# Three edits of order at the stage boundaries of a two-layer latent-token backbone

## The chip, the cores and the metric

The kernel runs on one core of a Trainium2 chip, in one launch. The metric is the device time of that launch in microseconds (us): 2392.98 us is the median of three runs of the kernel before (2392.16 to 2393.1). A core has TensorE (PE in the views; its weight loads are PEld), VectorE (DVE), ScalarE (ACT), GpSimd (POOL) and SyncE (SP), which issues the DMAs. Matrix products land in PSUM, which this kernel uses as eight banks of 128 x 512 float32; everything else is in SBUF.

## What is computed

Two layers work on 512 latent tokens of 1024 features; the first layer also takes 256 context tokens. Each layer is: half a feed-forward, a token mixer, half a feed-forward, each with a modulation before it and a normalization after it.

```python
def modulate(x, m, k):
    return x * (1 + m[..., 3 * k + 1, :]) + m[..., 3 * k, :]

def post_norm_update(x, y, m, k, g, b):
    return layer_norm(DN_ALPHA * x + m[..., 3 * k + 2, :] * y, g, b)

def swiglu(h, w_in, w_out):
    gate, up = jnp.split(h @ w_in, 2, axis=-1)
    return (jax.nn.silu(gate) * up) @ w_out

def macaron_half_ffn(x, m, k, w_in, w_out, g, b):
    return post_norm_update(x, 0.5 * swiglu(modulate(x, m, k), w_in, w_out), m, k, g, b)
```

The mixer of layer 0 (HGRN2) projects the modulated tokens to queries, values, two forget gates and an output gate, runs a gated recurrence in both directions over chunks, and multiplies by an output matrix. The mixer of layer 1 (the channel mix) is

```python
    u, v = jnp.split(jax.nn.gelu(h @ w_in), 2, axis=-1)
    v = layer_norm(v, v_g, v_b)
    v = jnp.einsum('gts,bnsgc->bntgc', w_s, v) + b_s.T[None, None, :, :, None]
    return (u * v.reshape(bsz, length, CM_INNER)) @ w_out
```

with 3072 features in u and in v (the reshapes of v are left out here).

## The kernel before

**Exact products from split numbers.** [...] `split` (L142, L143) cuts a float32 operand into a high part, which ScalarE rounds (L142), and a low part, which VectorE gets by subtraction (L143). `mm3` makes a product of three matmuls: high by high (L155), high by low (L156), low by high (L157). A weight block of 128 x 1024 is loaded into `raw` and split into `w`, of which there are six buffers.

**Fewer products by sums.** A 2 x 2 scheme of blocks with seven products in the place of eight is used for most layers (`seven`, L698, and its like). It needs sums and differences of weight blocks (L693 to L696, and L742 to L752 in its early form), and of operand blocks (`sum_steps`: L663, in the mixer's values L968), each of which is split too. The split operand sums are called f5, f6, f7 and f4 after the product that takes them. The products stand in PSUM banks psc, pse, psa, psb; ScalarE copies some of them out (L761).

**Boundaries.** An out-phase (`OutPhase.run`) sums y over the hidden features, adds the residual and normalizes each tile of 128 tokens (`evac`, `norm`: L379 to L418; the reciprocal root is taken on POOL, L408). Then `operand(p, kb)` makes one piece of the next phase's operand: four transposes on TensorE (L428) into a bank pt, the modulation on VectorE and ScalarE (L440, L438), and a split. p is the pair of tiles, kb the pair of feature blocks. The next phase has its first weights ready and takes the pieces one at a time (`staged`): for FeedSums that is 4 outputs x 2 blocks x 3 matmuls = 24 matmuls into four banks psf that are held until the last piece. With eight pieces there are operands o0 to o7 and held sums s0 to s7. o0 and o1 stand first, then the last products of y; the rest is written out by hand in the string `order` (L561), which the loop at L531 follows. GateIn, the way into the channel mix, has a string of its own (L1027). FeedSums stages f2, f3 and f4 take the default.

Behind that, `FeedSums.rest` sends the first group of `seven` with the four operand sums (`early`), and all of it that VectorE does stands behind the split that came last in the text, which is the one of o7:

```python
            if early:
                with tc.issue_after(latest[0].ins):
```

**The order on an engine.** The text gives each instruction a rank. When the program is built, a planner walks through it with estimated times: an engine takes the instruction of the best rank that is ready by these estimates, so later work can move ahead of earlier work that is not ready. The order is then fixed, and on the chip an engine follows it and waits where it must. `tc.issue_after(x)` adds an edge: what is issued inside it on x's engine stands behind x. `latest[0]` is the VectorE half of the last split.

**The first boundary** is `BothOut.run`: six tiles (four latent, two context), then the values of the mixer (`HgrnValues`). After the last y, o of pair 0 is there; `plain((0, 1))` makes two products for each of tiles 0 and 1 (pva, then pvc), `fifth` the weight differences, then come the operands of pairs 1 and 2, 32 transposes, and `plain((2,))`. The products of sums follow in `HgrnValues.rest`.

**The channel mix** makes the 24 blocks of u two at a time: j = 0 and 22 plainly, the others by `by_sums(j)` (`seven` without `early`), and after each pair `spatial`, with the products by w_s (L1969) and three steps on VectorE (L1975 to L1983). Before the change `by_sums` stands behind `ready`, the last of a row of normalizations on ScalarE, so the edge binds ScalarE's instructions alone.

Of the kernel before, what the change touches and what calls it, by code (L numbers as in the profile page):

```python
# [21 lines left out]
KD = D // P  # L22
# [53 lines left out]
def backbone_kernel(  # L76
# [38 lines left out]
    def swap(name, bufs=1):  # L115

        return sbuf(name=name, bufs=bufs, side="right")
# [9 lines left out]
    def bank(name):  # L127
        return psum.tile([P, 512], F32, tag="ps", name=name)
# [10 lines left out]
    latest, latest_hi, latest_load = [None], [None], [None]  # L139
# [126 lines left out]
    def operand_cols(l, j, nl, nj, cond):  # L266

        g, b = lnT[:, l, j, 0, :], lnT[:, l, j, 1, :]
        sc, sh = made((nl, 3 * nj + 1, cond)), made((nl, 3 * nj, cond))
        c = const.tile([P, 2, KD], F32, tag="opc", name="opc", bufs=2)  # L270
        nc.vector.tensor_tensor(c[:, 0, :], g, sc, ALU.mult)
        nc.vector.tensor_tensor(c[:, 1, :], b, sc, ALU.mult)
        nc.vector.tensor_tensor(c[:, 1, :], c[:, 1, :], sh, ALU.add)
        return c
# [281 lines left out]
    class Phase:  # L556
# [1 line left out]

        whole, later = False, iter(())
        hold = True  # L560
        order = "o2 o3 s0 s1 o4 o5 s2 o6 o7 s3 s4 s5 s6 s7"  # L561

        def load(self):
            pass
# [309 lines left out]
    class HgrnValues(Phase):  # L874
# [65 lines left out]
        def summed(f, i):  # L940
            return lambda k: (f[:, 0, k, i * P : (i + 1) * P], f[:, 1, k, i * P : (i + 1) * P])

        def plain(self, toks):

            for t in toks:
                pa, self.pc[t] = bank("pva"), bank("pvc")
                self.product(pa, [self.ws[2], self.ws[3]], self.of(1, t), True, True)
                self.product(self.pc[t], [self.ws[0], self.ws[1]], self.of(0, t), True, True)
                v = self.v[0][t]
                nc.scalar.activation(v, self.pc[t], AF.Copy)  # L950
                nc.vector.tensor_tensor(v, pa, v, ALU.add)
# [71 lines left out]

    class GateIn(Forms, Phase):


        order = "o2 o3 s0 s1 s2 o4 o5 s3 o6 o7 s4 s5 s6 s7"  # L1027

        def __init__(self, xm, new_block):
            self.xm = xm  # L1030
# [218 lines left out]
    class BothOut(OutPhase):  # L1249
# [30 lines left out]
        def run(self, bp, hl, nmod):  # L1280
            self.bp, self.hl, nt, npair, nxt = bp, hl, self.nt, self.npair, self.nxt
            flat = xmp.tile([P, 2, KD, T], F32R, tag="xm", name="hs").rearrange("p i k t -> p (i k t)")
            n = 2 * TA
            slots = [flat[:, i * n : (i + 1) * n].rearrange("p (i t) -> p i t", i=2) for i in range(2 * KD * T // n)]
            slots += [hl.tile([P, 2, TA], F32R, name=f"hs{i}") for i in range(2)]
            self.ring = cycle(slots)
            self.xs, self.st = [], []

            def done(p):
                for t in (2 * p, 2 * p + 1):  # L1290
                    self.evac(1, t)
                    self.norm(t)

            self.lead(0, 2, nmod)
            for t in range(nt):
                xt = bp.tile([P, D], F32, tag="x", name="x", bufs=nt)
                nc.sync.dma_start(xt, x[t] if t < NT else ctx_tok[t - NT])
                self.xs.append(xt)
                self.st.append(bp.tile([P, 2, 6], F32, tag="st", name="st", bufs=nt))
                self.lead(0, 3 + t, nmod)  # L1300
            self.lead(0, npair - 2, nmod)
            self.load_gate(0)
            held = [(kk, *self.operands(0, kk)) for kk in range(npair - 2, npair)]
            for t in range(nt):
                for h in held:
                    self.part(0, *h, [t])
                self.evac(0, t)
            self.load_gate(1)
            self.lead(1, npair - self.tail, nmod)
            held = [(kk, *self.operands(1, kk)) for kk in range(npair - self.tail, npair)]  # L1310
            self.both = [operand_cols(0, 0, 0, 1, n) for n in ("x", "c")]
            nxt.open(self.swapped())
            nxt.load(3)
            nxt.first = [hl.tile([P, TA], F32, tag="hl", name="hl", bufs=3) for _ in range(3)]
            nxt.first.append(nxt.u[1][1])
            for t in range(nt):
                for h in held:
                    self.part(1, *h, [t])
                if t % 2:
                    done(t // 2)  # L1320
                if t == 3:
                    for kb in range(KD // 2):
                        self.operand(0, kb)
            nxt.place()
            nxt.load(1)
            nxt.plain((0, 1))
            nxt.fifth()
            for p in range(1, nt // 2):
                for kb in range(KD // 2):
                    self.operand(p, kb)  # L1330
            nxt.copy_first()
            nxt.plain((2,))
            for t in range(NT):
                nc.sync.dma_start(self.xdst(t), self.xs[t])
# [549 lines left out]
    with ExitStack() as vhp_stack:  # L1884
# [8 lines left out]
        with sbuf(name="cm", bufs=1) as cm, ExitStack() as late:  # L1893
# [42 lines left out]
            def normalize(gi, t):  # L1936
                v = vs[gi][:, t, :]
                off, rstd = stat[t]
                return nc.scalar.activation(v, v, AF.Identity, scale=rstd, bias=off)
# [46 lines left out]
            for j in range(0, 3 * NG, 2):  # L1986
                for i in (j, j + 1):
                    if i % 3 == 0:
                        hs.append(vhp.tile([P, 3, T], F32, tag="vh", name="ht"))
                if j == 0:  # L1990
                    ready = [normalize(gi, t) for gi in range(2) for t in range(NT)][-1]
                if 0 < j < 3 * NG - 2:
                    with tc.issue_after(ready.ins):
                        us = by_sums(j)
                    gi = -(-(j + 2) // 3)
                    if gi > 1 and 3 * gi < j + 4:

                        for t in range(NT):
                            with tc.issue_after(gin.copies[t].ins):
                                normalize(gi, t)  # L2000
                else:
                    us = plain(j), plain(j + 1)
                if j == 3 * NG - 2:
                    gin.place.close()
                    mods = ExitStack()
                    modp = mods.enter_context(swap("modp4"))
                    op.release = mods.close
                for i, u in enumerate(us):
                    if j + i == 3 * NG - 1:
                        op.lead(0, 2)  # L2010
                    spatial(j + i, u)
# [96 lines left out]
```

## Time and profile before

| | |
|---|---|
| runs of the kernel before | 2392.16, 2392.98, 2393.1 us |
| the profiled execution's own time | 2393.77 us |
| its span, first to last instruction | 2392.1 us |
| mean granted TensorE clock | 0.999 |
| HBM traffic over the span | 150 GB/s |

| stretch (us from the span's start) | what stands there |
|---|---|
| 509 to 557 | the first boundary, from the feed-forward of both streams to the mixer's values |
| 926 to 965 | the boundary into f2 |
| 1276 to 1323 | the boundary into f3 |
| 1619 to 1655 | the boundary into GateIn |
| 1770 to 1890 | the channel mix's u by sums |
| 2027 to 2075 | the boundary into f4 |

In the rows of a timeline the first number is the start, the second the duration, both in us; then engine, line, operation, out<-in with shapes, a count, and in brackets the idle time of the engine before it and what ended that. A matmul's duration is longer than the step to the next matmul, since they run in a pipeline: time on TensorE is counted from start to start. In the view of waits a row names who waited, for what, how long in total, how often, and the longest.

### The profile page before, as it was taken

The numbers are of one execution on the slowest core, as the hardware profiler recorded it, in microseconds if no ns is written. First come the engines' busy times: TensorE is split into PE (matmuls) and PEld (weight loads), VectorE is DVE, ScalarE is ACT, GpSimd is POOL, SyncE is SP. The second block draws the span as 40 slices with busy tenths as digits, with TensorE's granted clock in tenths as the row PEclk, the third lists the DMA queues.
The fourth block names the chain that finished last, engine by engine and source line by source line (L and its number), as shares of the span: only waits on it lengthen the run. The fifth ranks groups of instructions, "written<-read, shape, count | busy, mean of one in ns | idle before, by whom it ended". The sixth has DMA issues, their size and how long they took to land.

```text
span 2392.1 us, 37772 instructions
## 1 busy us (share of the span) xinstructions
PE 2375.5 (99%) x14807; PEld 2184.2 (91%) x14807; DVE 1987.2 (83%) x3077; ACT 1243.2 (52%) x2054; POOL 45.5 (2%) x58
## 2 busy tenths in 40 slices
PE   9999999999999999999999999999999999999998
PEld 7999998888888888999989999889999988999987
DVE  8987896868787767988897988888888787988786
ACT  4544443336666653655544655544666543555641
POOL 0000000000000000000000000000000000000000
PEclk9999999999999999999999999999999999999999
DMA  8544489833222124433673333763322374333452
GB/s 336 185 156 133 141 293 358 301 137 115 80 89 71 53 63 141 155 106 107 206 252 130 117 107 115 218 207 132 108 95 84 126 263 148 124 116 103 146 164 72
DMA packets 110341, 362.08 MB, mean 151 GB/s; under 512 B 12697, under 2 KB 14801, under 8 KB 110162
## 3 DMA queue, kind: packets, MB, share of 16 engines
q1 hardware_dynamic: 110162, 359.66, 45.0%
q8 instruction: 116, 1.90, 0.3%
q14 instruction: 63, 0.52, 0.1%
HBM read 336.25 MB, written 23.36 MB: 150 GB/s over the span
## 4 chain that ended last, share of the span: by engine, by line
PE 92%; DVE 5%; DMA 1%; issue 1%; ACT 1%; POOL 0%; SPq 0%; DVEq 0%; POOLq 0%; ACTq 0%
PE y L155 9%; PE y L156 9%; PE y L157 9%; PE psc L155 7%; PE psc L157 7%; PE psc L156 7%; PE pse L157 3%; PE pse L155 3%; PE pse L156 3%; PE psf L157 2%; PE psf L156 2%; PE psf L155 2%; PE psa L156 2%; PE psa L155 2%; PE psa L157 2%; PE psf L1373 1%
## 5 line engine op out<-in xcount | busy, mean ns | idle before, releaser
L142 ACT ACTIVATE w<-raw 128x1024 fp32r<-128x1024 f32 (+2 forms) x384 | 363.7, 950 | 365.0 <-DMA raw<-in_ffn_w_out 148.6
L143 DVE TENSOR_TENSOR w<-raw,w 128x1024 fp32r<-128x1024 f32 (+2 forms) x384 | 416.3, 1088 | 99.1 <-ACT w L142 97.1
L155 PE MATMUL y<-w,hs 128*128 128x512 f32 x976 | 380.7, 390 | 0.0
L157 PE MATMUL y<-w,hs 128*128 128x512 f32 x976 | 379.8, 389 | 0.0
L156 PE MATMUL y<-w,hs 128*128 128x512 f32 x976 | 379.8, 389 | 0.0
L155 PEld LDWEIGHTS y<-w,hs 128*128 128x128 f32 x976 | 183.3, 188 | 38.2
L157 PEld LDWEIGHTS y<-w,hs 128*128 128x128 f32 x976 | 183.2, 188 | 38.3
L156 PEld LDWEIGHTS y<-w,hs 128*128 128x128 f32 x976 | 183.3, 188 | 37.4
L155 PE MATMUL psc<-f,w 128*128 128x256 f32 (+1 forms) x680 | 199.3, 293 | 0.0
L157 PE MATMUL pse<-f,w 128*128 128x256 f32 (+1 forms) x680 | 198.8, 292 | 0.0
L155 PE MATMUL pse<-f,w 128*128 128x256 f32 (+1 forms) x680 | 198.7, 292 | 0.2 <-ACT sc L761 0.2
L157 PE MATMUL psc<-f,w 128*128 128x256 f32 (+1 forms) x680 | 198.6, 292 | 0.0
L156 PE MATMUL pse<-f,w 128*128 128x256 f32 (+1 forms) x680 | 198.5, 292 | 0.0
L156 PE MATMUL psc<-f,w 128*128 128x256 f32 (+1 forms) x680 | 198.5, 292 | 0.0
L761 ACT ACTIVATE sc<-psc 128x256 f32<-128x256 f32 (+1 forms) x235 | 94.9, 404 | 149.9 <-PE psc L157 135.6
L155 PE MATMUL psc<-xm,w 128*128 128x256 f32 x548 | 156.2, 285 | 1.5 <-ACT sc L761 1.5
L157 PE MATMUL psc<-xm,w 128*128 128x256 f32 x548 | 155.0, 283 | 0.0
L156 PE MATMUL psc<-xm,w 128*128 128x256 f32 x548 | 155.0, 283 | 0.0
L143 DVE TENSOR_TENSOR w<-rawu,w 128x1024 fp32r<-128x1024 f32 x85 | 103.9, 1223 | 47.7 <-ACT w L142 47.6
L155 PEld LDWEIGHTS psc<-f,w 128*128 128x128 f32 x680 | 130.0, 191 | 1.1 <-ACT sc L761 0.9
L155 PEld LDWEIGHTS pse<-f,w 128*128 128x128 f32 x680 | 130.0, 191 | 0.4 <-ACT sc L761 0.4
L157 PEld LDWEIGHTS pse<-f,w 128*128 128x128 f32 x680 | 130.0, 191 | 0.3 <-DVE w L143 0.2
(447 smaller groups left out, 6167.2 us busy)
## 6 DMA issues: line engine op xcount, KB each, us to landing
raw<-in_ffn_w_in SPq DMA_DIRECT2D x109, 512.0 KB, 4.5
raw<-in_ffn_w_out SPq DMA_DIRECT2D x88, 512.0 KB, 4.2
rawu<-in_ffn_w_in SPq DMA_DIRECT2D x75, 512.0 KB, 3.6
rawu<-in_mod_w SPq DMA_DIRECT2D x72, 512.0 KB, 4.1
mraw<-in_mod_w SPq DMA_DIRECT2D x56, 512.0 KB, 5.2
hl<-hd SPq DMA_DIRECT2D x44, 384.0 KB, 5.5
raw<-in_hg_wf SPq DMA_DIRECT2D x32, 512.0 KB, 3.6
x<-x SPq DMA_DIRECT2D x28, 512.0 KB, 4.0
```

The lines of the kernel that those rows point to most:

```text
L142: latest_hi[0] = nc.scalar.activation(dst_hi, src, AF.Copy)
L143: latest[0] = nc.vector.tensor_tensor(dst_lo, src, dst_hi.bitcast(F32), ALU.subtract)
L155: nc.tensor.matmul(ps, ah, bh, start=start, stop=False, **kw)
L156: nc.tensor.matmul(ps, ah, bl, start=False, stop=False, **kw)
L157: return nc.tensor.matmul(ps, al, bh, start=False, stop=stop, **kw)
L761: self.copies.append(nc.scalar.activation(sc[i], ps[:, :N2], AF.Copy, scale=scale))
L1373: nc.tensor.matmul(f0.pss[u], a[:, u * P : (u + 1) * P], b, start=k + i == 0, stop=k == KD - 1 and i == 2)
```

## The change

Three edits; no arithmetic is changed, only the order of the work.

1. The default `order` becomes the one that GateIn has: the held sum s2 stands ahead of o4 and o5, s3 ahead of o6 and o7. GateIn's own string goes.
2. At the first boundary the four operands of pair 1 (`second`, 16 transposes) are issued between the two products of tile 1. `plain` gets a hook, `between`, for it. The operands of pair 2 stay behind `fifth`.
3. In the channel mix `by_sums(j)` gets a second edge: its instructions on VectorE stand behind the last split before it, which is that of the pair before.

```diff
@@ -558,7 +558,7 @@
-        order = "o2 o3 s0 s1 o4 o5 s2 o6 o7 s3 s4 s5 s6 s7"
+        order = "o2 o3 s0 s1 s2 o4 o5 s3 o6 o7 s4 s5 s6 s7"
@@ -940,11 +940,12 @@
-        def plain(self, toks):
+        def plain(self, toks, between=lambda: None):
 
             for t in toks:
                 pa, self.pc[t] = bank("pva"), bank("pvc")
                 self.product(pa, [self.ws[2], self.ws[3]], self.of(1, t), True, True)
+                between()
                 self.product(self.pc[t], [self.ws[0], self.ws[1]], self.of(0, t), True, True)
                 v = self.v[0][t]
                 nc.scalar.activation(v, self.pc[t], AF.Copy)
@@ -1023,8 +1024,6 @@
     class GateIn(Forms, Phase):
 
-
-        order = "o2 o3 s0 s1 s2 o4 o5 s3 o6 o7 s4 s5 s6 s7"
 
@@ -1323,11 +1322,16 @@
             nxt.load(1)
-            nxt.plain((0, 1))
+            nxt.plain((0,))
+
+            def second():
+                for kb in range(KD // 2):
+                    self.operand(1, kb)
+
+            nxt.plain((1,), second)
             nxt.fifth()
-            for p in range(1, nt // 2):
-                for kb in range(KD // 2):
-                    self.operand(p, kb)
+            for kb in range(KD // 2):
+                self.operand(2, kb)
             nxt.copy_first()
             nxt.plain((2,))
@@ -1990,7 +1994,7 @@
                 if 0 < j < 3 * NG - 2:
-                    with tc.issue_after(ready.ins):
+                    with tc.issue_after(ready.ins), tc.issue_after(latest[0].ins):
                         us = by_sums(j)
```

## The prediction

> **What bounds the kernel now.** Sections 1 of the page first, then the view of who waited for whom on TensorE alone.
>
> ```profile
> span 2392.1 us, 37772 instructions
> PE 2375.5 (99%) x14807; PEld 2184.2 (91%) x14807; DVE 1987.2 (83%) x3077; ACT 1243.2 (52%) x2054; POOL 45.5 (2%) x58
> ...
> PE psb L1353 <- DMA crow<-in_cond: 2.3, 1, 2.3
> PE psc L155 <- ACT sc L761: 1.5, 1, 1.5
> PE pt L428 <- DVE x L418: 0.9, 2, 0.6
> PE pva L155 <- ACT xa L142: 0.8, 1, 0.8
> PE pt L428 <- ACT held L438: 0.6, 1, 0.6
> PE pt L428 <- DVE blocks L418: 0.2, 1, 0.2
> ```
>
> TensorE (PE) sets the end: it is busy 2375.5 of 2392.1 us, so all its idle time together is 16.6 us, 0.7% of the span. The change removes no matmul and adds none; all it can win is idle time, and the rows above are nearly all of it that has a name behind it. The first one (2.3 us) is the start of the kernel, which the change doesn't touch. The other five are exactly the places that the three edits address: 0.6 + 0.8 at the first boundary, 0.9 + 0.2 at the three boundaries that take the default order, 1.5 in the channel mix. That is 4.0 us, 0.17%. I take 0.2% (4.8 us) as what a measurement of this kernel can tell from no change. So the question is less what is won than what is late next; for that I read VectorE (DVE) in the stretches behind these places, in the view by windows (length, then busy us and count of PE, PEld, DVE, ACT, POOL, then the granted clock):
>
> ```profile
> 557.00:565.00 8.00, 8.00 (x36) 6.52 (x36) 7.95 (x13) 7.62 (x12) 0.00 (x0) 1.00 0.01 2
> 565.00:573.00 8.00, 8.00 (x36) 6.50 (x36) 8.00 (x10) 4.65 (x7) 1.96 (x4) 1.00 0.00 0
> ...
> 947.90:962.30 14.40, 14.40 (x121) 14.26 (x119) 13.99 (x24) 7.74 (x13) 0.00 (x0) 1.00 0.11 30
> 1298.10:1322.20 24.10, 24.10 (x203) 24.10 (x203) 24.07 (x39) 13.84 (x24) 0.00 (x0) 1.00 0.17 62
> 2050.60:2074.60 24.00, 24.00 (x202) 24.00 (x201) 23.96 (x38) 13.82 (x24) 0.00 (x0) 1.00 0.32 113
> ```
>
> Behind every one of these boundaries VectorE is full (24.07 of 24.10 us) beside a full TensorE. The clock is 1.00 in all of them. Two queues run side by side without slack there, and a delay on one is seen on the other as soon as the margin between them is gone.
>
> **Part 1: the third held sum (s2) ahead of o4 and o5.** It reaches the three stages of FeedSums (f2, f3, f4); GateIn has this order already. Rows of f3, by time:
>
> ```profile
> 1288.02 0.69 DVE L143 TENSOR_TENSOR xm<-h,xm 128x512 fp32r<-128x512 f32 x1
> 1290.37 0.33 PE L428 MATMUL pt<-ident,x 128*128 128x128 f32 x1 [0.62 <-DVE x L418]
> 1296.86 1.29 DVE L143 TENSOR_TENSOR xm<-h,xm 128x512 fp32r<-128x512 f32 x2 [1.16 <-ACT xm L142]
> 1298.07 1.22 DVE L143 TENSOR_TENSOR w<-raw,w 128x1024 fp32r<-128x1024 f32 x1
> 1309.21 0.28 PE L157 MATMUL psf<-xm,w 128*128 128x256 f32 x1
> 1309.33 0.28 PE L155 MATMUL psc<-xm,w 128*128 128x256 f32 x1
> ```
>
> What it wins: o4's first transpose waits 0.62 us for the last normalized tile (L418). With s2, 24 matmuls, first, that wait is covered: matmuls of this form follow each other after 0.12 us (1309.21, 1309.33), so s2 takes 2.88 us. Its own operand (o2's split) ends at 1288.71, before it would start at about 1289.5. So 0.6 is won in f3; in f4 and f2 by the same reading 0.3 and 0.2:
>
> ```profile
> 2042.79 0.44 PE L428 MATMUL pt<-ident,x 128*128 128x128 f32 x2 [0.26 <-DVE x L418]
> ...
> 939.99 0.69 DVE L143 TENSOR_TENSOR xm<-blocks,xm 128x512 fp32r<-128x512 f32 x1
> ...
> 961.66 0.69 DVE L143 TENSOR_TENSOR w<-e,w 128x512 fp32r<-128x512 f32 x1 [0.24 <-ACT w L142]
> 962.41 0.39 PE L157 MATMUL pse<-f,w 128*128 128x256 f32 x1
> ```
>
> (In f2 o2's low half is ready only at 940.68, about 1 us after s2 would start; 16 of s2's 24 products need only the high half, 1.9 us of work, so I price that wait at nothing.)
>
> What it costs: every later step moves, and o6 and o7 too: they now stand behind s3, so five held sums are left behind their transposes before and four after. TensorE reaches the first weight-sum product 2.88 us sooner after o7 than now. What has to be ready by then hangs on o7: line 738 ties the whole chain of `seven` (weight split, four operand sums, their splits) behind o7's split, and the rows say so: w<-raw starts at 1298.07, the moment o7's L143 ends. From there VectorE doesn't rest for 24 us, so nothing can be pulled forward. The chain's margins to TensorE are:
>
> ```profile
> 1311.84 1.22 DVE L143 TENSOR_TENSOR w<-rawu,w 128x1024 fp32r<-128x1024 f32 x1
> 1315.33 0.28 PE L157 MATMUL pse<-f,w 128*128 128x256 f32 x1
> ...
> 1321.07 1.22 DVE L143 TENSOR_TENSOR w<-e,w 128x1024 fp32r<-128x1024 f32 x1
> 1322.41 0.32 PE L157 MATMUL pse<-f,w 128*128 128x256 f32 x1
> ```
>
> The first split of u ends at 1313.06 and is used at 1315.33: margin 2.27. The next group's split of e ends at 1322.29 and is used at 1322.41: margin 0.12. In f2 the split of e ends at 962.35, its use is at 962.41: 0.06. Taking 2.88 us from margins of 0.1 costs between nothing (if the planner finds other products for TensorE to run meanwhile) and 2.8 us a stage. It finds some: of 12 matmuls of a product 8 don't need the low half of the weights, 0.96 us, once or twice in the stretch. I take 1.6 for f3 and f4 (2.8 less one such filler and part of another), and 1.2 for f2, where the late item is e, computed last for its load, so that it may move up in VectorE's order. Net: f3 +1.0, f4 +1.3, f2 +1.0, together **+3.3 us**; ends: -1.1 (all cover holds) and 3 x 2.8 - 1.1 = +7.3.
>
> [...]
>
> **Part 2: tile transposes between the second tile's products.** Rows of the first boundary:
>
> ```profile
> 537.70 0.39 PE L155 MATMUL pvc<-w,xa 128*128 128x512 f32 x1
> ...
> 540.35 0.81 DVE L418 TENSOR_SCALAR x<-x,mv,rstd 128x1024 f32<-128x1024 f32 x1 [0.44 <-POOL rstd L408]
> 541.08 1.22 DVE L997 SCALAR_TENSOR_TENSOR ve<-vu,raw 128x1024 f32<-128x1024 f32 x1
> 543.40 1.77 PE L428 MATMUL pt<-ident,x 128*128 128x128 f32 x12 [0.63 <-ACT held L438]
> 546.01 0.50 PE L155 MATMUL pva<-w,xa 128*128 128x512 f32 x1 [0.84 <-ACT xa L142]
> ...
> 565.17 0.95 DVE L143 TENSOR_TENSOR f<-held,f 128x768 fp32r<-128x768 f32 x1
> 565.27 0.39 PE L155 MATMUL pvc<-w,f 128*128 128x512 f32 x1
> ```
>
> Now 32 transposes stand in one row behind the second tile's products; they run out of free PSUM banks (0.63) and then the third tile's product waits for its operand (0.84): 1.5 us shown. The first 16 move to 537.70, between the two products. Their operands are normalized (L418 of tile 5, needed by the last 16, ends at 541.16; those would start at about 542). Beside them VectorE's four evacuations run under the 2.7 us of the second product. They push work like the L997 at 541.08 (1.22 us, not needed before the second group of products) to later. Both waits should go: -1.5, up to -2.1 with the restarts. But VectorE is full from 557 to 573 (7.95 of 8.00, 8.00 of 8.00) and its split of f6 starts at 565.17, 0.1 us before TensorE's first product of f6. VectorE's work up to there is the same as before, so part of what is won arrives as a wait there: none of it lost, or all. The nearest row, the 0.1 margin, speaks for a loss, the pushed-back fillers and the one-sided products against. I take **-1.2**; ends -2.1 and +0.5.
>
> **Part 3: channel mix's sums behind the current splits.** The late period of the loop over j, and two loads from the chain that ended last:
>
> ```profile
> 1832.75 0.69 DVE L693 TENSOR_TENSOR e<-raw,rawu 128x512 f32<-128x512 f32 x1 [2.94 <-DMA rawu<-in_cm_wu]
> 1839.93 0.42 ACT L1957 ACTIVATE u<-u 128x256 f32<-128x256 f32 x1 [1.84 <-DVE u L1956]
> 1840.67 0.39 PE L155 MATMUL psc<-xm,w 128*128 128x256 f32 x1 [1.51 <-ACT sc L761]
> ...
> 1815.46 3.58 DMA rawu<-in_cm_wu
> 1827.43 5.30 DMA rawu<-in_cm_wu
> ```
>
> The next pair's first weight sum (L693) stands in VectorE's queue ahead of the current pair's split and of the sums on PSUM, and waits 2.94 us for its load, which took 5.30 us here and 3.58 in the period before. Behind it L1956 is late, behind that ScalarE's gelu (L1957), behind that the copy L761, for which TensorE stands 1.51 us. With the new edge L693 stands behind the current pair's last split; by then its load is long in. The wait leaves VectorE and the chain above has no head. The three sums are pushed by most of a period, but a pair's weights are split a period before use. **-1.5**; ends -1.7 (with the restart) and +0.5 if the later sums make a split late. As one load was slow in this execution, a part of this may not stand in the median.
>
> **Sum.** -1.2 + 3.3 - 1.5 = +0.6 on the profiled execution's own 2393.77 us. That execution is 0.79 above the median of 2392.98, so for the median I predict 2392.98 + 0.6 = **2393.6 us**: no change that can be told.
>
> **Rivals.**
> - *All cover holds* (the planner fills the shorter stretch): only the idle time goes, -1.1 - 1.5 - 1.5 = -4.1, 2388.9 us; with the restarts a little under 2388.2. For it: the planner puts other products where a split is late. Against: VectorE's 24.07 of 24.10. Chance 0.17, of which 0.07 below -0.2%.
> - *VectorE's full queue passes the whole shift on*: 7.3 at the three stages, nothing won at the first boundary, -1.5 in the channel mix: +5.8, **2398.8 us**, slower. It decides wherever a margin is under 2.88 us and no product is at hand. For it: margins of 0.06 and 0.12. Against: the fillers. Chance 0.08, of which 0.07 above +0.2%.
> - *The edits do less than they say*: the planner's order in the channel mix hardly matters without the slow load (0 instead of -1.5): +2.1, 2395.1 us. Chance 0.07.
>
> The forecast itself has 0.68. The range 2389.0 to 2397.6 leaves out what lies under the first rival's time and over +0.19%, about 2 in 10 at most. Faster by over 0.2%: 0.07; within: 0.86; slower: 0.07.
>
> **What would show it.** Right in part 1: at f3 and f4 no wait of pt for L418, 24 matmuls of psf more ahead of o4, and new idle time of PE on psc, pse or psb behind DVE's L143 some 15 to 25 us after o7; wrong: no such waits. Part 2: 16 transposes between pva and pvc of the second tile and no waits of 0.63 and 0.84; a wait of pve or pvc near 555 to 565 if VectorE takes it back. Part 3: L693 behind the split of 128x512 and no DMA wait on it; PE idle under 0.2 us from 1770 to 1900. A time under 2388 would say that the full queue behind o7 doesn't matter; one over 2398 that nothing fills it.

## The result, and the profile after

| | runs | median, us | lowest to highest |
|---|---|---|---|
| kernel before, beside it | 6 | 2393.14 | 2392.16 to 2394.33 |
| changed kernel | 6 | 2406.04 | 2404.65 to 2409.39 |

The ratio is 1.0056, with a 95% interval of 1.0045 to 1.0066; the medians lie 12.9 us apart. So the change costs time. Forecast were 2393.6 us, and 2397.6 as the upper end of the range: the measured time is 12.4 us over the forecast and 8.4 us over the range.

The profiled execution took 2407.65 us, 1.6 above the median. First the section on engines of its page (busy us, share, instructions):

```profile
span 2405.9 us, 37779 instructions
...
PE 2380.1 (99%) x14807; PEld 2187.1 (91%) x14807; DVE 1986.1 (83%) x3077; ACT 1242.6 (52%) x2054; POOL 44.9 (2%) x58
```

The span grew by 13.8 us. TensorE's idle time is 2405.9 - 2380.1 = 25.8 us, 9.2 more than the 16.6 of before. The other 4.6 us are in the busy time: the same 14807 matmuls took longer. So there are two things to find, new waits, and a slower TensorE. The waits come from the view of who waited for whom (us in total, times, longest):

```profile
PE pse L155 <- ACT w L142: 5.5, 3, 1.9
...
PE psc L155 <- ACT u L761: 2.2, 1, 2.2
PE psc L155 <- ACT sc L761: 1.6, 3, 1.1
...
PE psc L155 <- ACT w L142: 0.8, 2, 0.4
...
PE pve L157 <- DVE f L143: 0.4, 1, 0.4
```

Gone are the two waits of pt for L418, and the 1.5 of psc. New are three waits of pse of nearly 2 us for a split of weights, one in each of f2, f3 and f4; one of 2.2 us in the channel mix; and 0.4 at the first boundary. The 1.1 us for L761 stands at the start of the kernel (111 us), which the change doesn't touch; the last section comes back to it.

**Where the 2.88 us went in f3.** Rows of VectorE, TensorE and ScalarE:

```profile
1298.45 0.99 DVE L440 TENSOR_SCALAR h<-pt,opc 128x256 f32<-128x256 f32 x2 [2.10 <-PE pt L428]
...
1305.55 1.22 DVE L143 TENSOR_TENSOR w<-raw,w 128x1024 fp32r<-128x1024 f32 x1
...
1327.28 0.68 DVE L695 SCALAR_TENSOR_TENSOR e<-rawu,raw 128x512 f32<-128x512 f32 x1
...
1316.82 0.28 PE L155 MATMUL pse<-f,w 128*128 128x256 f32 x1
...
1327.99 1.06 ACT L142 ACTIVATE w<-e 128x1024 fp32r<-128x1024 f32 x1 [0.24 <-DVE e L695]
...
1329.10 0.39 PE L155 MATMUL pse<-f,w 128*128 128x256 f32 x1 [1.77 <-ACT w L142]
```

and the first and the last two of them in the kernel before:

```profile
1290.96 0.99 DVE L440 TENSOR_SCALAR h<-pt,opc 128x256 f32<-128x256 f32 x2
...
1319.65 1.06 ACT L142 ACTIVATE w<-e 128x1024 fp32r<-128x1024 f32 x1 [1.09 <-DVE e L695]
...
1320.85 0.30 PE L155 MATMUL pse<-f,w 128*128 128x256 f32 x1
```

With s2 ahead of o4, VectorE has nothing to do for 2.10 us until o4's transposes are there; before, it went straight on. Behind o7's split (1305.55) it has as much to do as ever. Call **distance** the time from that w<-raw to TensorE's first product on an operand sum (pse<-f): before 1312.21 - 1298.07 = 14.14 us, now 1316.82 - 1305.55 = 11.27. It is shorter by 2.87, the 24 matmuls of s2. VectorE reaches the second group's e (L695) at 1327.28, ScalarE rounds its high half from 1327.99 on, and TensorE has waited 1.77 us for that. In the kernel before the same high half was done at 1319.65 + 1.06 = 1320.71, and TensorE took it at 1320.85: the margin was 0.14 us. The wait is on L155, the first of the three matmuls of a product, so it is the high half that is late, and all 12 matmuls of the product stand behind it.

**Why TensorE was slower.** The view by windows of 1 us (length, busy us and count of PE, PEld, DVE, ACT, POOL, then the granted clock, DMA share, GB/s), f2 and then f4:

```profile
965.00:966.00 1.00, 0.00 (x0) 0.00 (x0) 0.96 (x3) 0.15 (x1) 0.00 (x0) 1.00 0.00 0
966.00:967.00 1.00, 0.47 (x2) 0.30 (x2) 1.00 (x2) 0.90 (x2) 0.00 (x0) 0.89 0.70 94
...
969.00:970.00 1.00, 1.00 (x7) 1.00 (x7) 1.00 (x2) 0.20 (x1) 0.00 (x0) 0.50 1.00 410
970.00:971.00 1.00, 1.00 (x9) 1.00 (x9) 0.96 (x3) 1.00 (x3) 0.00 (x0) 0.91 0.99 406
971.00:972.00 1.00, 1.00 (x11) 1.00 (x10) 1.00 (x3) 1.00 (x2) 0.00 (x0) 1.00 1.00 389
...
2086.00:2087.00 1.00, 1.00 (x9) 1.00 (x7) 1.00 (x2) 1.00 (x2) 0.00 (x0) 0.67 1.02 393
...
2089.00:2090.00 1.00, 1.00 (x7) 1.00 (x7) 0.75 (x2) 0.33 (x1) 0.00 (x0) 0.62 0.82 319
```

Behind the stalls of f2 and f4 the clock is 0.50, and a window of 1 us counts 7 matmuls and not 11. From the means of the edge windows it falls at 966 + 1 - 0.11/0.5 = 966.78 and is back at 970 + 0.09/0.5 = 970.18; in f4 from 2086.34 to 2089.76. In that stretch of f4 16 matmuls, from 2086.36 to 2089.77, follow each other after 0.21 us and not 0.12: 3.41 us for 1.92, so 1.5 us lost each time, by estimate from these steps. (The 1.7 of the expectations is half of 3.4.) Behind the equal stall of f3 (1.77 us) and the longer one of the channel mix (2.18) it stayed at 1.00.

### The profile page after: what moved, and what is told of

Its sections match the earlier page's. It is cut to its first block, busy times and chain, and to the rows that moved or that the text cites. A ratio compares the mean times of both kernels' runs of the same rounds, so it can differ in the third digit from the quotient of the medians.

```text
span 2405.9 us, 37779 instructions
## 1 busy us (share of the span) xinstructions
PE 2380.1 (99%) x14807; PEld 2187.1 (91%) x14807; DVE 1986.1 (83%) x3077; ACT 1242.6 (52%) x2054; POOL 44.9 (2%) x58
## 4 chain that ended last, share of the span: by engine, by line
PE 92%; DVE 5%; DMA 1%; ACT 1%; issue 1%; POOL 0%; SPq 0%; DVEq 0%; POOLq 0%; ACTq 0%
PE y L156 9%; PE y L157 9%; PE y L155 9%; PE psc L155 7%; PE psc L157 7%; PE psc L156 7%; PE pse L157 4%; PE pse L155 4%; PE pse L156 4%; PE psa L155 2%; PE psa L157 2%; PE psa L156 2%; PE psf L156 2%; PE psf L157 2%; PE psf L155 2%; PE psfl L155 1%
## 5 line engine op out<-in xcount | busy, mean ns | idle before, releaser
L142 ACT ACTIVATE w<-raw 128x1024 fp32r<-128x1024 f32 (+2 forms) x384 | 363.6, 950 | 372.1 <-DMA raw<-in_ffn_w_out 144.2
L143 DVE TENSOR_TENSOR w<-raw,w 128x1024 fp32r<-128x1024 f32 (+2 forms) x384 | 416.5, 1088 | 99.7 <-ACT w L142 97.4
L155 PE MATMUL y<-w,hs 128*128 128x512 f32 x976 | 381.0, 390 | 0.0
L157 PE MATMUL y<-w,hs 128*128 128x512 f32 x976 | 380.1, 389 | 0.0
L155 PEld LDWEIGHTS y<-w,hs 128*128 128x128 f32 x976 | 183.3, 188 | 38.5
L157 PEld LDWEIGHTS y<-w,hs 128*128 128x128 f32 x976 | 183.2, 188 | 37.9
L155 PE MATMUL pse<-f,w 128*128 128x256 f32 (+1 forms) x680 | 199.9, 294 | 5.5 <-ACT w L142 5.5
L155 PE MATMUL psc<-f,w 128*128 128x256 f32 (+1 forms) x680 | 199.9, 294 | 3.8 <-ACT u L761 2.2
L157 PE MATMUL pse<-f,w 128*128 128x256 f32 (+1 forms) x680 | 200.2, 294 | 0.1
L157 PE MATMUL psc<-f,w 128*128 128x256 f32 (+1 forms) x680 | 199.1, 293 | 0.0
L761 ACT ACTIVATE sc<-psc 128x256 f32<-128x256 f32 (+1 forms) x235 | 94.8, 403 | 153.0 <-PE psc L157 138.6
L155 PE MATMUL psc<-xm,w 128*128 128x256 f32 x548 | 156.5, 286 | 0.8 <-ACT w L142 0.8
L157 PE MATMUL psc<-xm,w 128*128 128x256 f32 x548 | 155.4, 284 | 0.3 <-DVE w L143 0.3
L143 DVE TENSOR_TENSOR w<-rawu,w 128x1024 fp32r<-128x1024 f32 x85 | 104.1, 1224 | 51.3 <-ACT w L142 51.2
L155 PEld LDWEIGHTS pse<-f,w 128*128 128x128 f32 x680 | 130.9, 193 | 6.1 <-ACT w L142 6.1
L155 PEld LDWEIGHTS psc<-f,w 128*128 128x128 f32 x680 | 130.5, 192 | 5.1 <-ACT sc L761 2.6
L157 PEld LDWEIGHTS pse<-f,w 128*128 128x128 f32 x680 | 131.2, 193 | 0.6 <-DVE w L143 0.4
```

Of the source, the lines that this page charges most:

```text
L142: latest_hi[0] = nc.scalar.activation(dst_hi, src, AF.Copy)
L143: latest[0] = nc.vector.tensor_tensor(dst_lo, src, dst_hi.bitcast(F32), ALU.subtract)
L155: nc.tensor.matmul(ps, ah, bh, start=start, stop=False, **kw)
L157: return nc.tensor.matmul(ps, al, bh, start=False, stop=stop, **kw)
L761: self.copies.append(nc.scalar.activation(sc[i], ps[:, :N2], AF.Copy, scale=scale))
```

## The experiments

Each kernel was measured against the kernel before on the same chip, with 5 or 11 runs of it and 14 to 33 of the kernel before. Times are medians; the ratio is to the kernel before.

| run | us | before, us | ratio, 95% interval |
|---|---|---|---|
| part 1 alone | 2403.02 | 2392.83 | 1.0042, 1.0030 to 1.0055 |
| part 2 alone | 2392.90 | 2392.83 | 1.0000, 0.9991 to 1.0009 |
| part 3 alone | 2395.66 | 2392.83 | 1.0010, 1.0001 to 1.0019 |
| s2 early, o7 kept | 2397.70 | 2392.83 | 1.0019, 1.0010 to 1.0028 |
| o7 late, s2 kept | 2403.98 | 2392.82 | 1.0043, 1.0031 to 1.0056 |
| part 1, weights freed | 2393.35 | 2392.82 | 1.0001, 0.9992 to 1.0010 |
| part 3 from the third pair | 2392.44 | 2392.82 | 0.9997, 0.9988 to 1.0006 |
| s2 in halves | 2395.41 | 2392.82 | 1.0011, 1.0002 to 1.0020 |
| part 2, copies on ScalarE | 2391.93 | 2393.05 | 0.9995, 0.9987 to 1.0004 |
| the change, repaired | 2393.46 | 2393.05 | 0.9999, 0.9990 to 1.0008 |
| weights freed, part 3 late | 2394.41 | 2393.05 | 1.0005, 0.9996 to 1.0013 |
| halves, weights freed, part 3 late | 2393.00 | 2393.05 | 0.9999, 0.9990 to 1.0008 |
| part 1, stall filled | 2402.68 | 2393.58 | 1.0039, 1.0025 to 1.0053 |
| part 2 on ScalarE, part 3 late | 2390.67 | 2393.58 | 0.9988, 0.9979 to 0.9998 |

### The three parts alone

Part 1 alone: the diff's first and third hunk.

> Part 1 alone (the held sums' order; the other two parts undone). Theory A, o7's place: VectorE's chain of weight split, operand sums and splits starts when o7's split is done, and TensorE now reaches its first weight-sum product 2.88 us sooner behind o7. So f2, f3 and f4 each show about 2.5 to 3.5 us of idle TensorE on pse and psc behind ScalarE and VectorE splits, one stall of 1.8 to 2.0 us among them, and where the granted clock falls to 0.50 behind it 1.7 us more. The time is 9 to 11 us above the kernel before (2402 to 2404). Theory B, the loss belongs to the three parts together or to the start of the kernel: under +6 us (below 2399).

Part 2 alone: its second and fourth hunk.

> Part 2 alone (tile transposes between the second tile's products). Theory A, from the trace of the changed kernel: the waits 0.63 + 0.84 go, but the second 16 transposes wait for banks again (0.63) and a product of the first operand sum waits for VectorE's split (0.37), so the time is within 0.5 us of the kernel before. Theory B, as predicted: 1.2 us faster.

Part 3 alone: its last hunk.

> Part 3 alone (channel mix's weight sums behind the current splits). Theory A, from the trace of the changed kernel: the wait of 1.51 late in the loop goes and one of 2.2 appears at its start, where the second pair's sums no longer use VectorE's idle time before the first pair's splits: +0.4 us, between -0.5 and +1.5. Theory B, as predicted: 1.5 us faster.

Measured: +10.2, +0.1 and +2.8 us. They add up to 13.1, the change's 12.9: within what these intervals can tell (2 us and more) the parts don't help or hinder one another, and the loss is part 1's first, then part 3's. For part 1 theory A held, in the time and in the waits. For part 3 theory A had the mechanism and missed the size: the stall of 2.2 us is there. In the profiled execution the clock fell to 0.50 behind it too, and the mean granted clock of that run is 0.998; eight of its eleven runs have 0.999, as the kernel before has, and take 2395.15 us on average. So the stall alone costs about 2.3 us.

The profile of part 1 alone, to be held against that of the kernel before:

```profile
span 2401.3 us, 37777 instructions
...
PE 2378.6 (99%) x14807; PEld 2186.4 (91%) x14807; DVE 1986.2 (83%) x3077; ACT 1242.5 (52%) x2054; POOL 45.5 (2%) x58
```

Of 9.2 us more, 6.1 are idle time of TensorE (22.7 against 16.6) and 3.1 are busy time.

What the channel mix was before is seen in the windows from 1745 to 1900 us, for the kernel before, for part 2 alone, and for the changed kernel:

```profile
1745.00:1900.00 155.00, 153.49 (x1173) 148.74 (x1172) 133.04 (x213) 99.89 (x171) 4.57 (x8) 1.00 0.30 100
```

```profile
1745.00:1900.00 155.00, 155.00 (x1183) 150.48 (x1183) 134.55 (x215) 101.17 (x173) 4.57 (x8) 1.00 0.30 100
```

```profile
1745.00:1900.00 155.00, 152.82 (x1184) 149.77 (x1182) 129.51 (x208) 100.41 (x174) 4.19 (x9) 1.00 0.28 93
```

Part 2 alone has the channel mix of the kernel before, and TensorE is busy 155.00 of 155.00 us in it. The 1.51 us of idle time in the profile of before came with one load of 5.30 us. Over the nine profiles in which the channel mix is as before, TensorE's busy time in this window is 153.49 to 155.00 us, 154.6 on average: 1.51 us is the most that was seen, and about 0.4 us is what there is to win.

### What in part 1 costs

Part 1 moves two things, s2 ahead of o4 and o7 behind one more sum. The next two runs part them; parts 2 and 3 are undone in both.

```diff
-        order = "o2 o3 s0 s1 o4 o5 s2 o6 o7 s3 s4 s5 s6 s7"
+        order = "o2 o3 s0 s1 s2 o4 o5 o6 o7 s3 s4 s5 s6 s7"
```

> Parts 2 and 3 undone; the default order puts the held sum s2 ahead of o4 and o5 as in the change, but no sum between o5 and o6, so that three sums stand ahead of o6 and o7, and five behind them, as in the kernel before. Theory A, o7's place decides: the stalls on pse in f2, f3 and f4 are not there, the granted clock stays 1.00, the waits of o4's transposes for the last normalized tile (0.62, 0.26) are gone; 16 transposes in a row may wait up to 0.6 us for banks. Time within -1.5 and +1 us of the kernel before. Rival, a sum ahead of o4 is what leaves VectorE idle (2.1 us before o4's copies) and is paid for later: the stalls stay, +5 us or more.

```diff
-        order = "o2 o3 s0 s1 o4 o5 s2 o6 o7 s3 s4 s5 s6 s7"
+        order = "o2 o3 s0 s1 o4 o5 s2 s3 o6 o7 s4 s5 s6 s7"
```

> The counterpart of the run with s2 early and o7 kept: parts 2 and 3 undone, s2 stays behind o4 and o5 as in the kernel before, and s3 goes ahead of o6 and o7, so that four sums stand ahead of o7 and four behind it. Theory A, the distance from o7 to the first weight-sum product decides: that distance falls from 14.1 to 11.3 us in f3 (and alike in f2 and f4), so the stalls of part 1 alone are here too, about 2.6 us of idle time a stage, and o4's waits (0.62, 0.26) stay: 2402 to 2405 us. Rival, s2 ahead of o4 is what costs: no stalls, within 1 us of the kernel before.

The second run is clear: o7 alone one sum later costs 11.2 us. Its waits of TensorE in f3:

```profile
PE pse L155 <- ACT w L142: 1.8, 1, 1.8
PE pt L428 <- DVE x L418: 0.6, 1, 0.6
PE psc L155 <- ACT w L142: 0.4, 1, 0.4
PE psc L155 <- ACT sc L761: 0.2, 1, 0.2
PE psc L157 <- DVE w L143: 0.2, 1, 0.2
```

The first run (+4.9) has the stalls of the rival and is 0.1 us under its time; theory A, as it was written, failed. Its rows in f3:

```profile
1299.82 1.22 DVE L143 TENSOR_TENSOR w<-raw,w 128x1024 fp32r<-128x1024 f32 x1
...
1312.88 0.28 PE L155 MATMUL pse<-f,w 128*128 128x256 f32 x1
```

and its only wait there over 0.1 us:

```profile
PE pse L155 <- ACT w L142: 1.4, 1, 1.4
```

Counting sums was too coarse: with no sum between o5 and o6, the copies and splits of all four pieces stand in one row on VectorE (1294.50 to 1299.90, with 0.9 us in it in which it waits for ScalarE's halves), so o7's split ends later behind them. The distance is 13.06 us, 1.08 shorter, and the stall 1.4; f4 shows the same 1.4. The same holds for s2 cut in two, with 12 of its 24 products on each side of o4 and o5 (`staged` takes the outputs as an argument):

```diff
-        order = "o2 o3 s0 s1 o4 o5 s2 o6 o7 s3 s4 s5 s6 s7"
+        order = "o2 o3 s0 s1 a2 o4 o5 b2 o6 o7 s3 s4 s5 s6 s7"
...
-                    (self.operand if kind == "o" else nxt.staged)(*steps[int(i)])
+                    us = {"a": ((0, 1),), "b": ((2, 3),)}.get(kind, ())
+                    (self.operand if kind == "o" else nxt.staged)(*steps[int(i)], *us)
```

> Parts 2 and 3 undone; s2 is cut in two: 12 of its 24 products ahead of o4 and o5, 12 behind them, so that o7 keeps three sums ahead of it and five behind, and its transposes stand in a row with none before. Theory A: the waits of o4 for the last normalized tile (0.62 in f3, 0.26 in f4) go, since 12 products take 1.44 us, and the distance from o7 to the first weight-sum product stays 14.1 us, so no stall appears: 0 to 1.5 us faster than before. Rival, anything moved ahead of o4 takes from VectorE's chain: a stall on pse of 0.5 to 1.5 us in f2, f3 and f4, +1 to +4 us.

It was 2.6 us slower, as the rival had it, with 0.6 + 0.4 us of waits in f4 too. In f2 neither of these two runs has a stall of that kind. In f3 all runs so far show one pattern:

| run | distance, us | shorter by | TensorE's waits on pse and psc |
|---|---|---|---|
| before | 1312.21 - 1298.07 = 14.14 | | none over 0.1 |
| s2 in halves | 1311.60 - 1298.52 = 13.08 | 1.06 | 0.6 + 0.4 |
| s2 early, o7 kept | 1312.88 - 1299.82 = 13.06 | 1.08 | 1.4 |
| o7 late, s2 kept | 1316.24 - 1304.98 = 11.26 | 2.88 | 1.8 + 0.4 + 0.2 + 0.2 |
| part 1 alone | 1314.38 - 1303.12 = 11.26 | 2.88 | 1.8 + 0.4 + 0.2 + 0.2 |

What is taken from the distance comes back as idle time, nearly one for one (1.06 to 1.0, 1.08 to 1.4, 2.88 to 2.6).

The next run leaves part 1's order as it is and takes work out from behind o7.

```diff
             if early:
-                with tc.issue_after(latest[0].ins):
-                    g, u, e = raws()
-                    wg = weights(g)
+                g, u, e = raws()
+                wg = weights(g)
+                with tc.issue_after(latest[0].ins):
                     next(early)
```

> Part 1 alone, with the first weight split behind o7 (w<-raw, 1.22 us on VectorE, 1.04 on ScalarE, and its loads) taken out of the tie to o7's split, so that it can run while VectorE waits for o4's transposes (2.1 us idle there). Theory A, VectorE's chain behind o7 is too long by the shift: it is 1.22 us shorter, so the idle time falls by 1 to 1.5 us in each of f2, f3 and f4, and the granted clock stays 1.00: 2394 to 2399 us. Rival, the stalls hang on something else (the loads, the banks, ScalarE's queue): 2402 to 2404, as part 1 alone.

The loss went from 10.2 to 0.5 us, below the range expected, because the edit does more than was meant: `latest[0]` is by then the split of w itself, so the tie to o7 is gone for all that follows. Rows of f3:

```profile
1290.00 0.65 DVE L742 TENSOR_TENSOR e<-raw,rawu 128x512 f32<-128x512 f32 x1
...
1293.08 0.69 DVE L143 TENSOR_TENSOR w<-e,w 128x512 fp32r<-128x512 f32 x1
1293.68 0.69 DVE L746 TENSOR_TENSOR rawu<-rawu 128x512 f32<-128x512 f32 x1
1294.28 0.69 DVE L693 TENSOR_TENSOR e<-raw,rawu 128x512 f32<-128x512 f32 x1
1294.89 0.69 DVE L747 SCALAR_TENSOR_TENSOR e<-rawu,raw 128x512 f32<-128x512 f32 x1
...
1296.39 0.69 DVE L143 TENSOR_TENSOR w<-e,w 128x512 fp32r<-128x512 f32 x1
```

These six steps (4.1 us) and the split of w (1.22) now run ahead of o6's and o7's copies, where VectorE stood idle; behind o7 they stood in TensorE's way. No wait on pse is left in f3. ScalarE, which rounds the high half, was itself waiting for VectorE's e in the changed kernel (0.24 us in f3, 2.28 in f2). So the stalls hang on what VectorE has to do behind o7. How much of the gain is the split of w and how much the six other steps was not parted.

### Part 2: the place of the copies

In part 2 alone the moved transposes are at 539.14, and TensorE's later waits are 0.5 for a bank, 0.3 for the third tile's operand and 0.4 for a split (pve). Rows of that run, VectorE, ScalarE and TensorE:

```profile
541.73 0.81 DVE L418 TENSOR_SCALAR x<-x,mv,rstd 128x1024 f32<-128x1024 f32 x1 [0.44 <-POOL rstd L408]
542.45 1.90 DVE L440 TENSOR_SCALAR held<-pt,opc 128x256 f32<-128x256 f32 x4
...
543.03 1.02 ACT L438 ACTIVATE held<-pt,opc 128x256 f32<-128x256 f32 x2 [5.82 <-DVE held L440]
...
539.14 1.91 PE L428 MATMUL pt<-ident,x 128*128 128x128 f32 x16
```

The transposed tiles stay in their banks for over 3 us: VectorE's copies stand behind other work, and ScalarE, idle for 5.82 us, waits for VectorE's half. The experiment gives these copies to ScalarE:

```diff
-                if i:
+                if i or scalar:
                     nc.scalar.activation(xf[:, i, :], pt[:, i, :], AF.Identity, scale=g, bias=b)
...
                 for kb in range(KD // 2):
-                    self.operand(1, kb)
+                    self.operand(1, kb, True)
```

> Part 2 alone, with the copies of the moved transposes out of PSUM all on ScalarE. In part 2 alone these tiles stood in PSUM from 539.1 to 542.5: VectorE's copies are queued behind a weight sum (L997, 1.21 us) and a normalization that waits 0.44 us for GpSimd, and ScalarE, idle 5.8 us, waits for VectorE's half. Theory A, this queue is where part 2's gain went: the copies start at once, the second 16 transposes find free banks (0.5 gone), the third tile's product its operand (0.32 gone), the split for pve comes earlier (0.36 gone): the idle time between 530 and 600 us falls from 2.3 to 1.2 us or less, and the time is 0.5 to 1.2 us under part 2 alone (2392.9). Rival, VectorE and ScalarE are full up to 565 us anyway: the idle time stays between 1.9 and 2.5 us, wherever it shows, and the time too.

As theory A had it. The windows from 530 to 600 us, part 2 alone and then with this edit:

```profile
530.00:600.00 70.00, 68.78 (x316) 56.22 (x316) 59.96 (x89) 44.66 (x67) 6.54 (x10) 1.00 0.32 107
```

```profile
530.00:600.00 70.00, 69.93 (x323) 57.36 (x322) 59.27 (x85) 47.59 (x71) 6.54 (x10) 1.00 0.32 107
```

1.22 us of idle time became 0.07. The time is 1.1 under the kernel before; its interval reaches over 1, so the time alone would not show it.

### Part 3: the first pairs

Rows of the changed kernel at the start of the loop, VectorE, ScalarE, TensorE:

```profile
1774.28 1.23 DVE L143 TENSOR_TENSOR w<-raw,w 128x1024 fp32r<-128x1024 f32 x1 [4.12 <-ACT w L142]
...
1780.09 0.69 DVE L693 TENSOR_TENSOR e<-raw,rawu 128x512 f32<-128x512 f32 x1
...
1782.86 1.06 ACT L142 ACTIVATE w<-e 128x1024 fp32r<-128x1024 f32 x1 [3.46 <-DVE e L695]
1783.82 0.36 ACT L761 ACTIVATE u<-psc 128x256 f32<-128x256 f32 x1
...
1784.24 0.39 PE L155 MATMUL psc<-f,w 128*128 128x256 f32 x1 [2.18 <-ACT u L761]
```

VectorE is idle for 4.12 us ahead of the pair j = 2, and the sums of j = 4, which ran there before, now wait for the last split of j = 2 and begin at 1780.09. ScalarE's split of e waits 3.46 us for them, the copy L761 is queued behind it, and TensorE waits for the copy.

```diff
-                    with tc.issue_after(ready.ins), tc.issue_after(latest[0].ins):
+                    with tc.issue_after(ready.ins), tc.issue_after(latest[0].ins) if j > 4 else ExitStack():
```

> Part 3 alone, without the new edge for the first two of the loop's four pairs with sums (edge only for j over 4). Theory A: the stall of 2.2 us at the loop's start is that of the pair j = 4, whose sums ran in VectorE's idle time before; without its edge the stall is gone, and the channel mix idles as little as in the runs whose load was not slow (about 0.6 us without the steps between forms): within 0.7 us of the kernel before. Rival, the edge costs in every period: +1.5 us or more.

The stall is gone, as theory A had it: TensorE is busy 155.00 of 155.00 us from 1745 to 1900. The time is the kernel before's within what can be told (-0.4). All five kernels with the edge from the third pair on show 155.00 us there, against the 154.6 on average without it; that is the same 0.4.

### Repairs, and a version that is faster

> All three parts of the change with two repairs: the first weight split is free of the tie to o7, and channel mix's new edge holds only for j over 4. Theory A, the two causes found carry all of the loss (10.2 and 2.8 of 12.9 us): 2391.5 to 2394 us, within 1.3 us of the kernel before. Rival, the parts together cost something that each alone doesn't: 2395 us or more.

It holds: all three parts with the freed weights and the edge from j over 4 take 2393.46 us. So the 12.9 us hang on the tie to o7 and on the new edge of the first two pairs: with both loosened 0.4 is left, which can't be told from no change.

> The kernel before with its own orders, the first weight split freed of the tie to o7, and channel mix's edge for j over 4 (no other part of the change). Theory A: the kernel before has no stall behind o7 to win back, so only the channel mix's share shows, 0 to 0.8 us faster: 2391.5 to 2393 us. Rival, freeing the weights takes VectorE's time ahead of o7's copies and delays o7: 0.5 to 2 us slower.

> As the run before it, and s2 in halves around o4 and o5. Theory A: with the weights freed the margin behind o7 is over the shift of the halves (stalls of about 1.1 us a stage without it), so only the gain on o4's waits is left (0.62, 0.26): 0.5 to 1.5 us faster than the kernel before, 2391.3 to 2392.3 us. Rival, as in the halves alone, a stall on pse or psc stays in f3 and f4: 2393 us or more.

Neither wins. The first leans to the slow side (+1.4), where its rival had it, though its interval holds 1; the second is where the kernel before is, at its rival's time, but without the rival's stall (f3 has no wait on pse and 0.4 us on psf). What o4's waits are worth (0.9 us) can't be told in the time.

> The kernel before with part 2 (copies of the moved transposes on ScalarE) and part 3 from the third pair on; part 1 undone. Theory: the two gains add, 1.1 and 0.4 to 0.6 us: 1.0 to 2.0 us faster than the kernel before (2391.0 to 2392.0), with 1.0 us of idle time between 530 and 600 us and 1.9 in the channel mix. Rival, they meet in the noise of the start (loads that land by chance up to 2 us later): no difference over 0.5 us.

This one is faster than both kernels: -2.9 us, ratio 0.9988, interval 0.9979 to 0.9998, just clear of 1; its eleven runs took 2389.56 to 2392.38 us. Expected were 1.0 to 2.0 us. Its page:

```profile
span 2388.7 us, 37772 instructions
...
PE 2375.5 (99%) x14807; PEld 2184.3 (91%) x14807; DVE 1985.1 (83%) x3073; ACT 1244.7 (52%) x2058; POOL 45.4 (2%) x58
```

13.2 us of idle time, 3.4 less than before. TensorE is busy 70.00 of 70.00 us from 530 to 600 and 155.00 of 155.00 in the channel mix, 3.0 us more than in the profile of before; about 1.1 of these go back to the slow load of that profile. The gain is more than the 1.5 of the two parts alone (-1.1 and -0.4); with intervals 0.2% wide that is no contradiction, and the 1.5 is the more careful guess of it.

### The clock behind a stall

Part 1 alone lost 10.2 us, more than the whole shift. This run asks whether the halved clock is the rest.

```diff
+            if fill: product(pe, wg, 0, b11, True, True)
             product(pe, we, 0, self.f5, True, True)
...
-                    self.steps if f == first else None,
+                    self.steps if f == first else None, f == first + 1,
```

> Part 1 alone, with 12 more matmuls (1.44 us) in f2, f3 and f4 that stand right before the product that waits longest (pse of the second group) and whose result is overwritten by it: TensorE works in most of the stall of 1.8 to 2.0 us instead of standing idle. Theory A, behind such a stall the granted clock falls to 0.50 for 3.41 us in some of the stages and costs 1.7 us each time: with the stall filled the clock stays 1.00 from 15 us to the last 8 us, the product starts when it did, and the time is 1.5 to 3.5 us under part 1 alone (2403.0), in spite of 4.3 us more of matmuls. Rival, the halved clock is not bound to the idle time, or costs nothing in the end: 2402.5 us or more.

It fits the rival's number (2402.68), but decides little. In f3 and f4 the added products fill the stall, cost nothing, and the clock stays 1.00; but in f2 the wait (2.0 us) stands before the first group's product, which the edit doesn't reach, and there the clock falls to 0.50 again. Windows of f2 and of f3:

```profile
968.00:969.00 1.00, 0.99 (x4) 0.99 (x5) 1.00 (x2) 0.41 (x1) 0.00 (x0) 0.50 0.93 348
1328.00:1333.00 5.00, 4.89 (x41) 4.69 (x40) 5.00 (x7) 4.20 (x7) 0.00 (x0) 1.00 0.14 34
```

Against the kernel before on its own chip it is 9.1 slower where part 1 alone is 10.2; the two intervals overlap. Both profiles have one fall of the clock (in part 1 alone at f3's stall), so the two can't show what a fall costs. That a fall costs 1.5 us is an estimate from the rows of the changed kernel; that work in the stall prevents it was not settled.

The mean clock recorded with each run says a little more. Counting falls ahead of 2370 us (behind that, with TensorE's last matmul done, the clock falls once more, at 2386.72 in the kernel before and at 2400.38 in the changed one), the kernel before with none has 0.999, part 1 alone, part 3 alone and o7 late, s2 kept, with one each, have 0.998, and the changed kernel with two has 0.997. The changed kernel's runs with 0.997 take 2407.13 us on average (four runs), those with 0.998 2405.32 (two); part 3 alone takes 2396.50 with 0.998 (three runs) and 2395.15 with 0.999 (eight). These steps of 1.8 and 1.4 us fit a fall of 1.5. In part 1 alone four of five runs have 0.997 and are only 0.5 us over the fifth; with the stall filled four of five have 0.998, and the fifth, at 0.999, is not faster. So the runs lean to the cost and to the remedy, and prove neither.

## Why the prediction was wrong, by its own steps

**What bounds the kernel** held: TensorE sets the end, and the question was what is late next. So did the sign of the worry, a full VectorE behind o7.

**Part 1** was the failure: +3.3 forecast, +10.2 measured alone. The step that failed is the discount. It read small margins rightly (0.12 in f3, 0.06 in f2, against 2.88 us) and then took 1.6 and 1.2 us a stage, on the ground that 8 of the 12 matmuls of a product don't need the low half of the weights. But its margins are those of the low half (L143, L157). The high half was as tight, 0.14 us in f3, and the stalls are on it (L155 behind L142): 1.77 us in f3, with none of the 12 matmuls free to run. The products of psa, which don't need these weights, stand behind that matmul in the changed kernel's order (1329.68, after 1329.10). Waits on a low half are there too, but of 0.2 us in f3. So the idle time of a stage was the whole shift but for 0.3 us. That nothing could be pulled forward held behind o7 only: 5.3 us of VectorE's work could go ahead of it, as the run with the weights freed shows.

The upper end that the text gave for this part, +7.3, was near the idle time: 1.9 + 0.6 in f2, 1.8 + 0.4 + 0.2 + 0.2 in f3 and in f4 make 7.7, less the 1.1 won, 6.6.

What no step priced is the granted clock, which fell to 0.50 at one of these stalls in the profile of part 1 alone and behind two in the changed kernel, 1.5 us each by estimate, and, as a cost of part 1, what a stop takes beyond its idle time: at 1329.10 the first matmul lasts 0.39 us and not 0.28, and the next starts 0.23 us behind it and not 0.12. The idle time and one fall come to 8.1 of the 10.2 us; with two falls, as the clock of 0.997 in four of its five runs suggests, it would be 9.6. How what is left divides stays open. In f2 the hope that e "may move up" failed too: its wait is the longest (1.9), with ScalarE waiting 2.28 us for e (L742).

**Part 2** was -1.2 forecast, 0 measured alone. The step that failed is "beside them VectorE's four evacuations run under the 2.7 us of the second product". They are queued behind VectorE's own work until 542.45, so the banks come free no sooner. With the copies on ScalarE the forecast 1.2 us come as idle time (1.22 to 0.07); in the time they are 1.1, inside the noise.

**Part 3** was -1.5 forecast, +2.8 measured alone. Two steps failed. "A pair's weights are split a period before use" is not so for the second pair, j = 4, whose sums had been made in the idle time before the loop. And the 1.51 us of the profile of before were mostly chance, as the text itself warned in its last sentence: about 0.4 is the mean of nine profiles, and a sum that goes to the median should have taken no more.

**The rivals.** The second (the whole shift passed on, 2398.8) had the mechanism and a chance of 0.08; its price lacked the clock, the stops' own cost and part 3's own stall. The range ended at 2397.6, under it.

## What to carry to other kernels

When two engines are both full, measure the distance between the point where one releases the other's chain and the point where its result is needed. Here nearly every microsecond taken from it became idle time (2.6 of 2.88 us). Ask of each margin which half of an operand it is for: products that can do without one half don't help when the other is as late. Look for the idle time of the second engine ahead of that point: moving its work there (weights that need no operand) was worth more here than moving TensorE's. A transpose moved forward was worth here only as much as the copy that frees its bank (1.22 us of idle time became 0.07 with the copies on ScalarE), and an edge that mends a loop's steady state must be looked at in the first turns of the loop.

## What the runs showed of the hardware

Behind a wait of 1.8 to 2.2 us TensorE's granted clock was halved in some cases and not in others. It fell behind one stall of 1.95 us (f2 of the changed kernel), behind one of 1.77 (f4), behind 2.2 in part 3 alone; it did not behind 1.77 (f3) and 2.18 (channel mix) of the changed kernel. In part 1 alone it fell at f3's stall of 1.8 us, and not behind f2's of 1.9. Each time it was 0.50 for 3.4 us: 3.40 in f2 and 3.42 in f4 of the changed kernel, 3.42 in part 1 alone (from 1326.36) and in part 3 alone (from 1777.62). The time from a stall's end to the fall was not the same either: in f2 the stall ended at 966.53, 0.25 us ahead of the fall at 966.78, and in f4 at 2085.07, 1.27 us ahead of the one at 2086.34; in part 1 alone the clock fell some 0.3 us before TensorE went on (a mean of 0.68 from 1326 to 1327, with TensorE busy for 0.33 us of it). With TensorE's last matmul of the changed kernel done (it starts at 2397.00) the clock fell once more, at 2400.38 (a mean of 0.69 from 2400 to 2401), and was still 0.50 from 2404 to 2405. So the length of a stall alone does not tell whether the clock falls behind it; what does was not shown.

The start of the kernel differs by chance between runs of one and the same order: TensorE waited 1.1 us at 111 us in the changed kernel and 1.0 in part 2 alone, behind a load that ScalarE's queue waits for (2.18 us in the changed kernel, 1.20 in the kernel before), and not at all in part 1 alone. Differences of about 1 us between single profiles can be that.
